# Memory rows kept without their token factor: the factor moves from GpSimd to the keys and values, and the key weights come as whole rows

## The chip, the core and the metric

The kernel runs on one core of a Trainium2 chip, as one launch. The core has a matrix engine (TensorE, PE in the profile, with PEld for its weight loads), VectorE (DVE), ScalarE (ACT), GpSimd (POOL) and a queue engine (SyncE, SP) that here issues almost all DMAs. The metric is the device time of one execution in microseconds, lower is better. Of several runs the median is compared.

## What is computed

One step of a two-layer encoder trunk on 512 prompt tokens and 32 sample tokens, model width 1024. Layer 0 mixes tokens by an RWKV-7 recurrence, layer 1 by differential attention. Both layers also attend to a memory of 256 rows, and what matters for the change is how the keys and values of that memory are made:

```python
def rmsnorm(x, w):
    xf = x.astype(jnp.float32)
    y = xf * lax.rsqrt(jnp.mean(xf * xf, axis=-1, keepdims=True) + EPS)
    return (y * w.astype(jnp.float32)).astype(x.dtype)

def mem_kv(mem, norm_w, wk, wv):
    h = rmsnorm(mem, norm_w)
    return ((h @ wk).reshape(B, N_MEM, MEM_HEADS, MEM_HD),
            (h @ wv).reshape(B, N_MEM, MEM_HEADS, MEM_HD))
```

For each layer `mem` is the same 256 x 1024 matrix `mem_prompt`; `norm_w`, `wk` and `wv` (1024 x 512, four heads of 128) are the layer's own. Keys and values are outputs as well as operands of the attention. The factor `rsqrt(mean(x*x) + EPS)` is one number for each memory row (for each token of the memory), the same for both layers: this is the token factor of the title. It stands in front of a whole row, so it can be applied to the row before the product with `wk` or `wv`, or to the product after it.

## The kernel before

Everything is kept transposed: features on the 128 partitions, tokens along the free axis, so a 1024-wide row is eight tiles, `k` = 0 to 7. The products of the two layers run in a split precision: a weight tile is cast by ScalarE to `whi`, VectorE forms the rest `wlo` = raw - `whi`, and activations are split into `hh` and `hl` in the same way (for the memory `mmh` and `mml`). Three matmuls (`whi` with `hh`, `whi` with `hl`, `wlo` with `hh`) make one product.

All instructions but those of GpSimd go through the helper class `Queue` (L99 to L104), so nearly every row of the profile names L104, and rows are told apart by tile names. While `self.ordered` is true, `Queue` ties each instruction of an engine behind the one that the program issued before it on that engine: in the opening, and in layer 0, the order of the program text is the order of each queue. SP's queue holds the DMAs in program order too. An instruction that waits holds up everything behind it on its engine.

The opening, `inputs()` (L363 to L563), does this, in the order of its text:

- It issues the loads: the memory rows `xm` in two halves (`memory(0)`, `memory(1)`), the norm weights `pB`, the key weights of layer 0 in eight pieces (`keys(g, k)`: 256 rows by 256 columns, that is two tiles `k` for the two heads of group `g`), the sample rows, the four prompt tiles `xp` (tiles `xt` 3 to 6 of the profile's numbering by `square` and `scaled`), then weight blocks (`load`, tile `raw`, five buffers) and small parameters.
- PE transposes the memory rows (`turn(k)`, tile `ps_mt`). `taken(k)` makes two copies: VectorE writes `m` (in buffer `at`), multiplied by the norm weight of layer 0, and ScalarE writes the plain copy `mo` (in `bv` and `yt`), which layer 1 will use with its own norm weight. Neither has the token factor yet.
- `key(g, k)` multiplies the key weights with `m` in plain float32: four matmuls of 128x256 each call (two tiles `k`, two heads), accumulated in four PSUM tiles, two heads first and the other two after.
- `square(i, ...)` sums the squares of the token rows (ScalarE or VectorE), `roots(v)` turns the sums into factors `rs` with nine short VectorE instructions in a row (L461 and `rsqrt`, L129), once for tiles 0 to 4 and once for tiles 5 and 6, the last two prompt tiles. `scaled(i, ...)` multiplies the prompt rows with their factors. The memory's factors are not put on the rows: two diagonal tiles `dg` and a matmul with ones spread them along the free axis, ScalarE copies them to `rb` (in `rsb`), and `key_out(h)` multiplies the finished keys of head `h` with `rb`.
- `turned(k)` transposes the scaled prompt tiles, `normed(k)` makes `hh` and `hl` from them (ScalarE, then VectorE), and a loop over `k` runs the first weight block (`raw36`) in step with them, with `mem_out` for the four heads of keys between.

Then layer 0 begins (`layer0`, L1413): `lora_in`, `memory()` (L565 to L578), and the first three ordinary blocks. `memory()` is where GpSimd comes in:

```python
            self.nc.gpsimd.tensor_tensor(x, x, r2, ALU.mult)
            self.ae.copy(mh[:, f, :], x)
            self.nc.gpsimd.tensor_tensor(ml[:, f, :], x, mh[:, f, :].bitcast(F32), ALU.subtract)
        for k in range(4):
            self.nc.gpsimd.tensor_tensor(mo[k], mo[k], r2, ALU.mult)
            self.se.dma_start(self.mscr[k], mo[k])
```

The eight multiplications by `r2` (L572, L576) put the factor on `m` and `mo`; four subtractions (L574) make `mml`; and `mo` goes out to DRAM (`mscr`). GpSimd's instructions aren't tied to the program order, so each starts as soon as its own operands are there, also in the middle of the opening. Later the values of layer 0 are made from `mmh` and `mml` (`mem_block`, L1167), `mem_again` (L1117) loads `mo` back for layer 1, and `mem_kv` (L1153) makes keys and values of layer 1. `mem_out` (L1139) transposes a finished head on PE, ScalarE copies it to `memt`, and SP stores it.

## Time and profile before

| what | us |
|---|---|
| median of 3 runs | 1441.03 |
| lowest and highest of them | 1439.93, 1441.11 |
| the profiled execution, its own time | 1438.12 |
| span of that execution, first to last instruction | 1436.4 |
| PE busy in the span | 1390.6 |
| DVE busy | 924.8 |
| ACT busy | 828.5 |
| POOL busy | 389.2 |

The profiled execution took 1438.12 us, 2.9 us less than the median, and 1.7 us of it lie outside the span. All times of the trace below belong to this one execution and count from the start of its span. A row of a timeline gives the start, the length, the engine, the tile written and the tiles read, the shape, how many instructions the row joins, and in brackets how long the engine stood idle before and what ended that.

### The profile page before, as it was taken

The numbers are of one execution on the slowest core, as the hardware profiler recorded it, in microseconds if no ns is written. First come the engines' busy times: TensorE is split into PE (matmuls) and PEld (weight loads), VectorE is DVE, ScalarE is ACT, GpSimd is POOL, SyncE is SP. The second block draws the span as 40 slices with busy tenths as digits, with TensorE's granted clock in tenths as the row PEclk, the third lists the DMA queues.
The fourth block names the chain that finished last, engine by engine and source line by source line (L and its number), as shares of the span: only waits on it lengthen the run. The fifth ranks groups of instructions, "written<-read, shape, count | busy, mean of one in ns | idle before, by whom it ended". The sixth has DMA issues, their size and how long they took to land.

```text
span 1436.4 us, 31914 instructions
## 1 busy us (share of the span) xinstructions
PE 1390.6 (97%) x11877; PEld 1310.1 (91%) x11877; DVE 924.8 (64%) x2337; ACT 828.5 (58%) x2278; POOL 389.2 (27%) x850
## 2 busy tenths in 40 slices
PE   6999999999999998999999999999999999999997
PEld 5998899999999998988999999989999999999997
DVE  6666777777877877676743656564465746557533
ACT  4665677767676676565433456654465446664322
POOL 4226567565765567600000120000000001000100
PEclk9999999999999999999999999999999999999999
DMA  6443222332223232342554472323332223332321
GB/s 206 125 129 88 58 58 73 82 97 59 78 76 82 75 78 60 92 122 77 165 160 127 142 206 68 91 85 96 97 90 82 85 74 89 90 105 59 97 83 70
DMA packets 264773, 139.20 MB, mean 97 GB/s; under 512 B 57689, under 2 KB 254562, under 8 KB 264618
## 3 DMA queue, kind: packets, MB, share of 16 engines
q1 hardware_dynamic: 264618, 137.16, 34.0%
q8 instruction: 94, 1.54, 0.4%
q14 instruction: 61, 0.50, 0.1%
HBM read 110.98 MB, written 22.78 MB: 93 GB/s over the span
## 4 chain that ended last, share of the span: by engine, by line
PE 81%; DVE 7%; ACT 7%; DMA 2%; issue 2%; SPq 1%; DVEq 0%; ACTq 0%
PE ps_g L104 56%; PE ps_c L104 4%; PE ps_s L104 2%; PE ps_o L104 2%; PE ps_at L104 2%; PE ps_v L104 1%; DVE wlo L104 1%; PE ps_mo L104 1%; PE ps_mm L104 1%; PE ps_aT L104 1%; SPq L104 1%; PE ps_ss L104 1%; ACT whi L104 1%; PE ps_w L104 1%; DVE nt L104 1%
## 5 line engine op out<-in xcount | busy, mean ns | idle before, releaser
L104 PE MATMUL ps_g<-hh,wlo 128*128 128x272 f32 x1808 | 538.3, 298 | 2.7 <-DVE wlo L104 2.7
L104 PE MATMUL ps_g<-hh,whi 128*128 128x272 f32 x1808 | 537.5, 298 | 0.6 <-DVE qp L104 0.6
L104 PE MATMUL ps_g<-hl,whi 128*128 128x272 f32 x1808 | 531.6, 295 | 0.3
L104 PEld LDWEIGHTS ps_g<-hh,wlo 128*128 128x128 f32 x1808 | 341.5, 189 | 7.5 <-DVE wlo L104 3.6
L104 PEld LDWEIGHTS ps_g<-hh,whi 128*128 128x128 f32 x1808 | 342.2, 190 | 5.0 <-PE ps_g L104 0.8
L104 PEld LDWEIGHTS ps_g<-hl,whi 128*128 128x128 f32 x1808 | 341.8, 189 | 4.5 <-DVE hl L104 0.7
L104 DVE TENSOR_TENSOR wlo<-raw,whi 128x512 fp32r<-128x512 f32 x314 | 218.7, 709 | 190.4 <-ACT whi L104 187.0
L104 ACT CAST whi<-raw 128x512 fp32r<-128x512 f32 x314 | 190.2, 617 | 173.1 <-PE ps_g L104 99.7
L860 POOL TENSOR_TENSOR tm<-u,m 102x84 f32<-102x84 f32 (+23 forms) x341 | 147.2, 432 | 155.4 <-DMA m<-sc 129.6
L862 POOL TENSOR_TENSOR u<-u,tm 102x84 f32<-102x84 f32 (+23 forms) x341 | 147.0, 431 | 26.6
L104 PE MATMUL ps_g<-hi,wlo 128*128 128x272 f32 x512 | 147.8, 289 | 0.9 <-DVE wlo L104 0.9
L104 PE MATMUL ps_g<-hi,whi 128*128 128x272 f32 x512 | 148.6, 290 | 0.0
L104 PE MATMUL ps_g<-lo,whi 128*128 128x272 f32 x512 | 147.4, 288 | 0.0
L1312 POOL TENSOR_TENSOR lo<-og,hi 128x544 fp32r<-128x544 f32 x8 | 13.7, 1713 | 486.4 <-DVE og L104 351.3
L104 PEld LDWEIGHTS ps_g<-hi,wlo 128*128 128x128 f32 x512 | 96.3, 188 | 1.1 <-DVE wlo L104 1.1
L104 PEld LDWEIGHTS ps_g<-hi,whi 128*128 128x128 f32 x512 | 96.4, 188 | 0.0
L104 PEld LDWEIGHTS ps_g<-lo,whi 128*128 128x128 f32 x512 | 96.4, 188 | 0.0
L104 DVE SCALAR_TENSOR_TENSOR SB<-ps_c,dl,sd 64x64 f32<-64x64 f32 x168 | 47.5, 283 | 41.3 <-PE ps_c L104 36.1
L1731 POOL TENSOR_TENSOR hl<-hn,hh 128x544 fp32r<-128x544 f32 x8 | 11.8, 1479 | 210.4 <-ACT hh L104 210.4
L104 ACT COPY sv<-ps_c 64x64 f32<-64x64 f32 x192 | 39.3, 205 | 44.4 <-PE ps_c L104 42.7
L104 ACT ACTIVATE sg<-ps_g 128x272 f32<-128x272 f32 x64 | 25.3, 395 | 64.1 <-PE ps_g L104 59.9
L104 ACT ACTIVATE pt<-ps_s,snm 128x128 f32<-128x128 f32 (+3 forms) x96 | 50.7, 529 | 18.0 <-DVE snm L104 17.0
(387 smaller groups left out, 2622.0 us busy)
## 6 DMA issues: line engine op xcount, KB each, us to landing
raw<-in_rw_in_dram SPq DMA_DIRECT2D x114, 256.0 KB
raw<-in_df_in_dram SPq DMA_DIRECT2D x112, 256.0 KB
raw<-in_w_out_dram SPq DMA_DIRECT2D x64, 256.0 KB
oscr<-sg SPq DMA_DIRECT2D x16, 272.0 KB
lo<-oscr SPq DMA_DIRECT2D x16, 272.0 KB
m<-sc SPq DMA_DIRECT2D x33, 128.0 KB
raw<-in_w_mem_v_dram SPq DMA_DIRECT2D x16, 256.0 KB
kh<-kh SPq DMA_DIRECT2D x24, 136.0 KB
```

The costliest lines, as they stand in the source:

```text
L104: return lambda *a, **k: self.trunk.tie(self, issue(*a, **k))
L860: nc.gpsimd.tensor_tensor(tm[:, :n, :wd], u3[:, :n, kx : kx + 1].to_broadcast(sh), m3[:, kx : kx + 1, kx + 1 :].to_broadcast(sh), ALU.mult)
L862: nc.gpsimd.tensor_tensor(u3[:, :n, kx + 1 :], u3[:, :n, kx + 1 :], tm[:, :n, :wd], ALU.add)
L1312: (self.nc.gpsimd if g % 2 and self.o1 else self.ve).tensor_tensor(lo[:], t, hi[:].bitcast(F32), ALU.subtract)
L1731: nc.gpsimd.tensor_tensor(self.hl[:, k, :], h[:], self.hh[:, k, :].bitcast(F32), ALU.subtract)
```

## The change

- The token factor no longer goes onto the memory rows. `memory()` loses the eight multiplications on GpSimd, and `m` and `mo` stay without the factor. `mml` is now subtracted by VectorE, in four instructions, in the order of the program.
- What is made from those rows gets the factor afterwards. Values (`mem_out` with `kind == 1`): memory tokens are on the partitions there, so ScalarE's copy of 128x256 becomes two activations of 128x128 with a factor for each partition (`self.mrs`, the tile `rs`, now kept in the constant pool). Keys of layer 1 (`mem_kv` with `kind == 0`): the copy out of PSUM, on ScalarE before, is a VectorE product with the spread factors `self.rsb`. Keys of layer 0 had `key_out` already.
- `rb` is stored to DRAM (`rscr`) in the opening, and loaded again in `mem_again`, after the eight tiles of `mo`.
- The stores of `mo` to `mscr` are issued at the end of `inputs()`, ahead of the loads `up`.
- The key weights come as eight pieces of 128 whole rows by 512 columns, and `key(k)` runs all four heads for one tile `k`. The loads of pieces 2 to 6 stand behind the sample rows, between and behind the prompt tiles. All four `key_out` now stand together behind `normed(0)`.
- The two loads of `pB` are issued first, and by ScalarE's queue.

```diff
-            def keys(g, k):
-                self.se.dma_start(wm[4 * g + k], a["w_mem_k"][0][2 * k * P : 2 * k * P + 2 * P, 2 * g * P : 2 * g * P + 2 * P]
-                                  .rearrange("(k p) c -> p k c", p=P))
+            def keys(*ks):
+                for k in ks:
+                    self.se.dma_start(wm[k], a["w_mem_k"][0][k * P : k * P + P, :])
...
+            parB = self.params(p, "pB", [(a[n].rearrange("l (j p) -> (l j) p", p=P), 16) for n in ("norm_w", "mem_norm_w")], self.ae)
             memory(0)
-            parB = self.params(p, "pB", [(a[n].rearrange("l (j p) -> (l j) p", p=P), 16) for n in ("norm_w", "mem_norm_w")])
-            keys(0, 0)
             keys(0, 1)
             memory(1)
-            keys(0, 2)
-            keys(0, 3)
             self.se.dma_start(xs[:TS, :], a["x_sample"][0])
             prompt(0)
+            keys(2)
             prompt(1)
-            keys(1, 0)
+            keys(3)
             prompt(2)
-            keys(1, 1)
+            keys(4)
             prompt(3)
-            keys(1, 2)
-            keys(1, 3)
+            keys(5, 6, 7)
...
-            ss, rs = (p.tile([P, 7], F32, name=n) for n in ("ss", "rs"))
+            ss, rs = p.tile([P, 7], F32, name="ss"), self.c.tile([P, 7], F32, name="rs")
+            self.mrs = rs
+            self.rscr = self.dp.tile([P, NMEM], F32, name="rscr")
...
-            key_out(0)
-            key_out(1)
             normed(0)
+            for h in range(MH):
+                key_out(h)
             todo[3][0]()
+            self.se.dma_start(self.rscr[:], rb)
...
-    def memory(self, m, mo, rb):
+            for k in range(4):
+                self.se.dma_start(self.mscr[k], mo[k])
+        return m
+
+    def memory(self, m):
 
         mh, ml = self.mem_tiles()
-        r2 = rb.unsqueeze(1).to_broadcast([P, 2, NMEM])
-        for k in range(4):
-            f = slice(2 * k, 2 * k + 2)
-            x = m[:, f, :]
-            self.nc.gpsimd.tensor_tensor(x, x, r2, ALU.mult)
-            self.ae.copy(mh[:, f, :], x)
-            self.nc.gpsimd.tensor_tensor(ml[:, f, :], x, mh[:, f, :].bitcast(F32), ALU.subtract)
-        for k in range(4):
-            self.nc.gpsimd.tensor_tensor(mo[k], mo[k], r2, ALU.mult)
-            self.se.dma_start(self.mscr[k], mo[k])
+        for k in range(0, KT, 2):
+            f = slice(k, k + 2)
+            self.ae.copy(mh[:, f, :], m[:, f, :])
+            self.ve.tensor_tensor(ml[:, f, :], m[:, f, :], mh[:, f, :].bitcast(F32), ALU.subtract)
...
-        self.ae.copy(tok[:], ps[:, :256].rearrange("p (j c) -> p j c", j=2))
+        if kind == 0:
+            self.ae.copy(tok[:], ps[:, :256].rearrange("p (j c) -> p j c", j=2))
+        else:
+            for j in range(2):
+                self.ae.activation(tok[:, j, :], ps[:, j * P : j * P + P], AF.Copy, scale=self.mrs[:, j : j + 1])
...
-            self.gemm([self.weights(src, h * P)], [(mh, ml)], lambda ps, v: self.ae.copy(t[:], ps), cols=NMEM, parts=1)
+            self.gemm([self.weights(src, h * P)], [(mh, ml)], lambda ps, v: self.ve.tensor_tensor(t[:], ps, self.rsb[:], ALU.mult)
+                      if kind == 0 else self.ae.copy(t[:], ps), cols=NMEM, parts=1)
```

What this does to GpSimd's own queue, from the end of its first memsets to the first pair's inversion. `at` holds `m`, `bv` and `yt` hold `mo`, `rsb` the spread factors. Before:

```order
L572 TENSOR_TENSOR at_89<-at_89,rsb 128x512
L576 TENSOR_TENSOR bv_94<-bv_94,rsb 128x512
L576 TENSOR_TENSOR bv_95<-bv_95,rsb 128x512
L572 TENSOR_TENSOR at_89<-at_89,rsb 128x512
L576 TENSOR_TENSOR bv_102<-bv_102,rsb 128x512
L576 TENSOR_TENSOR yt_101<-yt_101,rsb 128x512
L572 TENSOR_TENSOR at_89<-at_89,rsb 128x512 x2
L1430 MEMSET raw_479 128x1
```

And in the changed kernel, between the same two neighbours:

```order
L1570 MEMSET yt_101 128x128
L1430 MEMSET raw_485 128x1
L1430 MEMSET raw_486 128x1
L212 IOTA t_508 128x640
L257 MEMSET bk 128x32 x2
```

All eight products are gone, and nothing stands in their place on this queue.

VectorE's queue in the opening, from the sample rows' `hl` on, the lines with a minus before and those with a plus now; `memk` are the keys of layer 0 as `key_out` writes them, `hl<-ps_t` is VectorE's half of `normed(k)`:

```order
 L104 TENSOR_TENSOR hl<-rsb,hh 128x8x32
-L104 TENSOR_TENSOR memk<-ps_g,rsb 128x256 x2
 L104 SCALAR_TENSOR_TENSOR hl<-ps_t,PB,hh 128x512
-L104 TENSOR_TENSOR wlo<-raw,whi 128x512
-L104 SCALAR_TENSOR_TENSOR hl<-ps_t,PB,hh 128x512 x2
-L104 TENSOR_TENSOR memk<-ps_g,rsb 128x256
-L104 SCALAR_TENSOR_TENSOR hl<-ps_t,PB,hh 128x512
+L104 TENSOR_TENSOR memk<-ps_g,rsb 128x256 x3
 L104 TENSOR_TENSOR memk<-ps_x,rsb 128x256
-L104 SCALAR_TENSOR_TENSOR hl<-ps_t,PB,hh 128x512 x2
+L104 TENSOR_TENSOR wlo<-raw,whi 128x512
+L104 SCALAR_TENSOR_TENSOR hl<-ps_t,PB,hh 128x512 x5
```

The four key products are now one group behind the first `hl`, ahead of `wlo` and the second `hl`; before, two stood ahead of the first and two further back.

VectorE's queue at the start of layer 0, in the changed kernel:

```order
L104 SCALAR_TENSOR_TENSOR tmp<-raw_485,PA,tmp 128x544
L104 TENSOR_TENSOR wlo<-raw,whi 128x512
L104 TENSOR_TENSOR lora_574<-tmp,lora_574 64x544
L104 TENSOR_TENSOR lora_575<-tmp,lora_575 64x544
L104 TENSOR_TENSOR mml<-at_89,mmh 128x512 x4
L104 SCALAR_TENSOR_TENSOR rkv<-raw_486,PA,rkv 128x544
L104 TENSOR_TENSOR wlo<-raw,whi 128x512
```

The four `mml` are the new rows; before, `rkv` followed `lora` directly, and GpSimd made `mml` beside it.

More of the change, by code (lines that the diff above doesn't have):

```diff
@@ L141, in rsqrt, with params @@
         self.ve.scalar_tensor_tensor(y, t[:], 5.0 * f ** 4, y, ALU.add, ALU.mult)
-    def params(self, p, name, rows):
+    def params(self, p, name, rows, queue=None):
         t = p.tile([P, P], F32, name=name)
@@ L444, in taken, with key @@
                 self.ae.copy(mo[k], v)
-            def key(g, k):
-                for j in range(2):
-                    for h in range(2):
-                        self.te.matmul(pk[2 * g + h][:, :NMEM], wm[4 * g + k][:, j, h * P : h * P + P], m[:, 2 * k + j, :],
-                                       start=k + j == 0, stop=2 * k + j == KT - 1)
+            def key(k):
+                for h in range(MH):
+                    self.te.matmul(pk[h][:, :NMEM], wm[k][:, h * P : h * P + P], m[:, k, :], start=k == 0, stop=k == KT - 1)
             def square(i, act):
@@ L491, in inputs @@
             taken(1)
-            key(0, 0)
+            key(0)
             square(0, True)
@@ L496, in inputs @@
             taken(2)
-            key(0, 1)
+            key(1)
             turn(3)
             taken(3)
-            key(0, 2)
-            key(0, 3)
+            key(2)
+            key(3)
             square(2, True)
@@ L525, in inputs @@
             todo[2][0]()
-            key(1, 1)
+            key(5)
             ps = self.psm.tile([P, 512], F32, tag="m", name="ps_ts")
@@ L537, in inputs @@
             self.ve.tensor_tensor(self.hl[:, :, TP:], hs, self.hh[:, :, TP:].bitcast(F32), ALU.subtract)
-            key_out(0)
-            key_out(1)
             normed(0)
+            for h in range(MH):
+                key_out(h)
             todo[3][0]()
+            self.se.dma_start(self.rscr[:], rb)
             self.early = [self.load(w, 0)]
@@ L1121, in mem_again @@
         for k in range(KT + 2):
-            if k < KT:
-                mo[k] = p.tile([P, NMEM], F32, tag="memo", name="mo", bufs=2)
-                self.se.dma_start(mo[k][:], self.mscr[k // 2][:, k % 2, :])
+            if k <= KT:
+                t = p.tile([P, NMEM], F32, tag="memo", name="mo", bufs=2)
+                self.se.dma_start(t[:], self.mscr[k // 2][:, k % 2, :] if k < KT else self.rscr[:])
+                if k < KT:
+                    mo[k] = t
+                else:
+                    self.rsb = t
             if 0 < k <= KT:
```

15 lines of the change are left out of this document (6 added, 9 removed).

## The prediction

> **What bounds the kernel now.** I read the page first, then PE's waits, then the stretches of the opening with the granted clock, then the timelines of PE, DVE, POOL and ACT there. The page says that PE is the engine to watch:
>
> ```profile
> span 1436.4 us, 31914 instructions
> PE 1390.6 (97%) x11877; PEld 1310.1 (91%) x11877; DVE 924.8 (64%) x2337; ACT 828.5 (58%) x2278; POOL 389.2 (27%) x850
> ```
>
> PE is idle for 1436.4 - 1390.6 = 45.8 us. A change that leaves PE's work as it is can win only from these, and from work that PE does at a low clock. The list of PE's waits names the largest (us in total, times, longest):
>
> ```profile
> PE ps_t L104 <- DVE xt L104: 6.4, 1, 6.4
> PE ps_g L104 <- DVE wlo L104: 3.6, 5, 1.1
> ```
>
> The first is one wait, for VectorE's scaled prompt tile. The table by stretches (length, then busy time of PE, PEld, DVE, ACT, POOL, then PE's granted clock, DMA share, GB/s) shows it, and what it costs afterwards:
>
> ```profile
> 24.00:30.19 6.19, 0.00 (x1) 0.01 (x1) 5.95 (x9) 0.81 (x1) 4.93 (x5) 0.69 0.17 50
> 30.19:34.00 3.81, 3.81 (x14) 3.23 (x15) 3.34 (x8) 2.42 (x5) 0.00 (x0) 0.60 0.33 103
> ```
>
> PE does nothing for 6.2 us, and in the 3.8 us after it the clock is 0.60. Why is VectorE late? Its timeline:
>
> ```profile
> 19.27 1.21 DVE L104 SCALAR_TENSOR_TENSOR sg<-xt 128x1024 f32<-128x1024 f32 x1
> 20.59 1.05 DVE L104 TENSOR_SCALAR ss<-ss 128x2 f32<-128x2 f32 x1
> 21.67 1.19 DVE L104 TENSOR_SCALAR rs<-ss 128x2 int32<-128x2 int32 x1
> ...
> 27.77 1.18 DVE L104 TENSOR_TENSOR nt<-nt,ss 128x2 f32<-128x2 f32 x1
> 28.99 0.16 DVE L104 SCALAR_TENSOR_TENSOR nt<-nt 128x2 f32<-128x2 f32 x1
> 29.18 0.16 DVE L104 SCALAR_TENSOR_TENSOR rs<-nt,rs 128x2 f32<-128x2 f32 x1
> 29.38 0.75 DVE L104 TENSOR_SCALAR xt<-xt,rs 128x1024 f32<-128x1024 f32 x1
> ```
>
> Nine instructions on two columns each make the factors of the last two prompt tiles. The last two take 0.16 us, the seven before them 1.05 to 1.19. POOL's timeline says what runs beside the slow ones:
>
> ```profile
> 19.81 1.79 POOL L572 TENSOR_TENSOR at<-at,rsb 128x512 f32<-128x512 f32 x1 [11.61 <-ACT rsb L104]
> 21.57 2.48 POOL L576 TENSOR_TENSOR bv<-bv,rsb 128x512 f32<-128x512 f32 x2
> ...
> 27.68 1.25 POOL L572 TENSOR_TENSOR at<-at,rsb 128x512 f32<-128x512 f32 x1
> ...
> 55.85 5.98 POOL L574 TENSOR_TENSOR mml<-at,mmh 128x512 fp32r<-128x512 f32 x4 [2.31 <-ACT mmh L104]
> ```
>
> From 19.81 to 28.93 POOL multiplies rows with the token factor, 1.25 us each, and each short DVE instruction lasts about as long as one of them, as if one were let through for each of POOL's. When POOL stops, DVE is back at 0.16. These are the instructions that the change removes.
>
> **Term 1, the gap.** What is next when POOL is silent? DVE's nine start at 20.59 and follow each other by 29.38 - 29.18 = 0.20 us: done at 22.4. DVE then scales one tile (0.75, to 23.2) and ACT the other:
>
> ```profile
> 18.13 1.15 ACT L104 ACTIVATE xt<-xt,rs 128x1024 f32<-128x1024 f32 x1 [0.30 <-DVE rs L104]
> ```
>
> that is to 23.6. PE's own timeline:
>
> ```profile
> 12.56 3.62 PE L104 MATMUL ps_g<-at,at 128*128 128x256 f32 x16
> ...
> 18.64 0.68 PE L104 MATMUL ps_rb<-dg,ones 128*128 128x128 f32 x4 [0.74 <-DVE dg L104]
> ...
> 23.43 0.38 PE L104 MATMUL ps_t<-ident,xt 128*128 128x128 f32 x2
> 30.19 1.72 PE L104 MATMUL ps_t<-ident,xt 128*128 128x128 f32 x6 [6.38 <-DVE xt L104]
> ```
>
> PE has key products until 23.43, so DVE and PE now arrive together, and PE goes on at about 23.8 instead of 30.19. Gain 6.4.
>
> **Term 2, the clock.** Without the gap the clock should stay at 1.00. PE's 3.81 us at 0.60 hold 3.81 x 0.60 = 2.3 us of work: gain 1.5.
>
> [...]
>
> **Term 3, the second collision.** At 55.85 POOL makes `mml`, and DVE is slow again; PE stands:
>
> ```profile
> 48.13 0.68 DVE L104 TENSOR_TENSOR wlo<-raw,whi 128x512 fp32r<-128x512 f32 x1
> ...
> 57.46 1.53 DVE L104 SCALAR_TENSOR_TENSOR rkv<-raw,PA,rkv 128x544 f32<-128x544 f32 x1 [1.50 <-ACT raw L104]
> 58.91 1.77 DVE L104 TENSOR_TENSOR wlo<-raw,whi 128x512 fp32r<-128x512 f32 x1
> ```
>
> ```profile
> 60.74 0.39 PE L104 MATMUL ps_g<-hh,wlo 128*128 128x272 f32 x1 [1.13 <-DVE wlo L104]
> ```
>
> `wlo` takes 1.77 us instead of 0.68. The change gives DVE the four subtractions itself. They have the form of `wlo` (128x512, both inputs in SBUF), 0.6 each back to back, and each waits for its cast:
>
> ```profile
> 55.15 2.19 ACT L104 CAST mmh<-at 128x512 fp32r<-128x512 f32 x4
> ```
>
> They begin when the second `lora` is done, 55.96, and end near 58.4. Behind them queue `rkv` and `wlo`, 0.7 each: 59.8 instead of 60.69. PE waits about 0.2 instead of 1.13: gain 0.9. If DVE were slowed by something else there it could be 0; it can't exceed 1.13.
>
> **Term 4, the keys in a bunch.** `key_out` times four stands ahead of the second `hl`. With PE starting its first `whi` step at 26.1 (23.8, six transposes 0.6, four key products 1.7), `key_out(3)` ends near 27.1, `wlo` 27.7, the second `hl` 28.4, where PE wants it at 27.6. Part comes back, since DVE has no key product inside the loop any more and the third `hl` comes at the same distance from the start as before (3.0 us): cost 0.4, between -0.5 and 0.8.
>
> **Term 5, the order of the loads.** Key rows 3 and 4 now follow prompt tiles 1 and 2. Those land here:
>
> ```profile
> 14.70 1.23 DVE L104 SCALAR_TENSOR_TENSOR sg<-xt 128x1024 f32<-128x1024 f32 x1 [1.25 <-DMA xt<-in_x_prompt_dram]
> ```
>
> ```profile
> 16.68 1.06 ACT L104 ACTIVATE junk<-xt 128x1024 f32<-128x1024 f32 x1 [0.40 <-DMA xt<-in_x_prompt_dram]
> ```
>
> Ahead of row 3 stand as many bytes as before ahead of prompt tile 1, so it lands near 14.7. PE (16 key matmuls from 12.56 are rows 2 and 3) wants it at 14.3. Row 4 lands near 16.7, wanted at 16.0. PE slips by 0.4 to 0.7, but it stands for 0.74 before `ps_rb` anyway. Cost 0.2, at most 1.1. No transfer grows; rows are 2 KB instead of 1.
>
> **Term 6, the small ones.** `pB` by ACT's queue is issued 0.9 us earlier, but PE waits only this long for it:
>
> ```profile
> 5.67 0.28 PE L104 MATMUL ps_par<-ident,pB 32*128 32x32 f32 x1 [0.22 <-DMA pB<-in_mem_norm_w_dram]
> ```
>
> Gain 0.2, between 0 and 0.22. On SP's queue the four `mscr` stores now pass ahead of `up`, some 2.5 us of issuing; `up` is wanted ten microseconds later, and the stores wait for nothing: 0. `rscr` is one issue ahead of a weight load, 0.35 us, waiting for `rb`, long there: 0. Each of eight `memt` becomes two instructions:
>
> ```profile
> L104 ACT COPY memt<-ps_mkt 128x256 f32<-128x256 f32 x16 | 5.9, 371 | 7.3 <-DMA mkv<-memt 3.8 <-PE ps_mkt L104 3.4
> ...
> L104 ACT ACTIVATE osT<-ps_osT,dv 128x128 f32<-128x128 f32 x3 | 1.1, 367 | 1.6 <-PE ps_osT L104 1.6
> ```
>
> At most 0.36 us more each, 2.9 together, on an engine that is 58% busy, and only a store waits for it. Cost 0.1, between 0 and 0.7.
>
> **Term 7, layer 1's keys.** Here the change adds waits: four `memx` on DVE, each held until PE has finished its block, with the whole DVE queue behind. DVE is nearly full there. Two of its groups, 816 to 834, while POOL makes `hl` (count, then busy us, mean ns, then idle before):
>
> ```profile
> L104 DVE TENSOR_TENSOR wlo<-raw,whi 128x512 fp32r<-128x512 f32 x11 | 11.0, 1032 | 0.4 <-ACT whi L104 0.4
> L104 DVE SCALAR_TENSOR_TENSOR hn<-x,PB,ps_r 128x512 f32<-128x512 f32 x8 | 5.9, 738 | 0.3 <-POOL hl L1731 0.3
> ```
>
> `hl` of the opening has `hn`'s form with POOL nearly silent, and `x`, from 760 to 811, has `memx`'s, one input in PSUM and one in SBUF:
>
> ```profile
> L104 DVE SCALAR_TENSOR_TENSOR hl<-ps_t,PB,hh 128x512 fp32r<-128x512 f32 x8 | 6.0, 748 | 5.7 <-ACT hh L104 5.5
> ```
>
> ```profile
> L104 DVE TENSOR_TENSOR x<-ps_g,x 128x272 f32<-128x272 f32 x8 | 3.5, 438 | 6.2 <-PE ps_g L104 6.2
> ```
>
> Beside POOL `wlo` goes from 0.68 to 1.03 us, and `hn`, at 738 against 748 ns, isn't slowed. I take 0.42 for each `memx`; slowed like `wlo` it would be 0.63. That is 1.7 to 2.5 us more on an engine that `wlo` and `hn` alone fill for 16.9 of 18 us. One of the four falls into this idle time, one into the 0.4 before `wlo`:
>
> ```profile
> 811.95 0.17 DVE L104 TENSOR_SCALAR tm_m<-ps_n 128x5 f32<-128x5 f32 x1 [1.03 <-PE ps_n L104]
> ```
>
> The other two push the rest by 0.4 each, and I put half of that on PE. Cost 0.4, between 0 and 2.
>
> [...]
>
> **The sum.** 6.4 + 1.5 + 0.9 + 0.2 - 0.4 - 0.2 - 0.1 - 0.4 = 7.9 us. After 62 us PE is the bound, and everything there is released by PE's progress, so I expect the shift to be kept to the end. The profiled execution's 1438.12 would be 1430.2. It was 2.9 below the median of the runs; taking the sum off the median, 1441.03 - 7.9 = 1433.1.
>
> **Rivals.**
> 1. *The loads set the opening.* If the rows 4 to 7, now last, come 3 to 4 us late, PE waits for `zr` instead of `xt`: gain 4.4, 1436.6. For it: the loads run at full share to 20 us; against: PE never waits for a key row now, and byte counts don't grow. 0.12.
> 2. *Layer 1's DVE queue, slower than before.* ACT's copies of these products, which DVE now makes, follow their blocks, some 3 us each (the third and the fourth):
>
> ```profile
> 820.10 0.37 ACT L104 COPY memx<-ps_g 128x256 f32<-128x256 f32 x1
> ...
> 822.65 0.37 ACT L104 COPY memx<-ps_g 128x256 f32<-128x256 f32 x1
> ```
>
> If each `memx` holds DVE for a whole block and PE then stands for `wlo`, four times 3 us and 0.8 for slowing make 12.8, net 4.9 slower: 1446. It decides from 7.9 us of PE idle between 811 and 835. Against it: in DVE's queue `memx` stands about where its block ends, so it should wait for tenths. 0.04.
> 3. *Given back.* If layer 0's stages are paced by weights or by SP's queue and not by PE, the opening's gain turns into waiting for `raw` before 130 us: 1441. Against: from 62 to 70 PE is full. 0.06.
> 4. *More.* The bunch of keys costs nothing, the loads with whole rows come faster, and the first loop, where DVE has less to do, shortens by 2: gain 11, 1430. 0.08.
>
> **The numbers.** The forecast has 0.70. The range reaches from 1429.0 (gain 10.5, and 1.5 for the spread of the runs shown, 3 us with the profiled one) to 1438.0 (rival 1 and 1.4 of spread); it leaves out rivals 2 and 3. A measurement of this kernel can tell about 0.2%, 2.9 us, from no change. Faster by more than that: forecast, rivals 1 and 4, 0.90; within it: rival 3, 0.06; slower: rival 2, 0.04.
>
> **What would show it.** In the profile after: the nine instructions at 0.16 to 0.2 each; no wait of PE for `xt` above 1 us; clock 1.00 from 24 to 34; the first `whi` step near 26; `wlo` at 0.7 near 50; PE idle in the layer-1 stage below 2 us. I am wrong if PE waits there for `zr`, `raw` or `wlo` instead, if the nine stay slow with POOL silent, or if the first 100 us are 8 us shorter and the end isn't.

## The result, and the profile after

The changed kernel takes 1433.11 us (median of 4 runs, 1432.36 to 1433.81) against 1440.55 (4 runs, 1439.93 to 1441.11): ratio 0.9948, 95% interval 0.9931 to 0.9966, 7.4 us less. The profiled execution took 1432.36. Of all runs below, one of experiment 6 took 1499.98 us at a granted clock of 0.847 and is left out of its ratio. Its page, in the lines that answer to those of before:

```profile
span 1430.4 us, 31910 instructions
PE 1391.5 (97%) x11877; PEld 1309.5 (92%) x11877; DVE 917.7 (64%) x2345; ACT 828.8 (58%) x2282; POOL 375.0 (26%) x838
```

PE's idle time fell from 45.8 to 38.9 us. In the list of PE's waits the largest of before, `xt` with 6.4, is gone; this line stands:

```profile
PE ps_g L104 <- DVE wlo L104: 3.3, 6, 0.9
```

VectorE's timeline has the nine short instructions (first and last) and the prompt tile behind them, PE's timeline the transposes of it and the first step of the loop; the last line is the first step before:

```profile
20.19 0.17 DVE L104 TENSOR_SCALAR ss<-ss 128x2 f32<-128x2 f32 x1
...
21.77 0.16 DVE L104 SCALAR_TENSOR_TENSOR rs<-nt,rs 128x2 f32<-128x2 f32 x1
21.96 0.75 DVE L104 TENSOR_SCALAR xt<-xt,rs 128x1024 f32<-128x1024 f32 x1
```

```profile
18.24 0.68 PE L104 MATMUL ps_rb<-dg,ones 128*128 128x128 f32 x4 [0.21 <-DVE dg L104]
...
23.02 1.04 PE L104 MATMUL ps_t<-ident,xt 128*128 128x128 f32 x8
...
25.94 0.63 PE L104 MATMUL ps_g<-hh,whi 128*128 128x272 f32 x2 [0.16 <-DVE memk L104]
```

```profile
34.01 0.60 PE L104 MATMUL ps_g<-hh,whi 128*128 128x272 f32 x2
```

The nine take 1.7 us instead of 8.8. PE makes eight transposes of the prompt tiles without a wait and begins the loop at 25.94, where before it began at 34.01. The table by stretches (columns as in the prediction) shows the granted clock, the seventh figure after the busy times, at 1.00:

```profile
24.00:26.00 2.00, 1.84 (x10) 1.32 (x8) 1.71 (x4) 1.26 (x3) 0.00 (x0) 1.00 0.26 78
26.00:30.00 4.00, 3.67 (x27) 3.36 (x28) 2.80 (x6) 1.34 (x2) 0.00 (x0) 1.00 0.78 228
```

The second collision, on VectorE's timeline:

```profile
48.53 2.50 DVE L104 TENSOR_TENSOR mml<-at,mmh 128x512 fp32r<-128x512 f32 x4
50.94 0.78 DVE L104 SCALAR_TENSOR_TENSOR rkv<-raw,PA,rkv 128x544 f32<-128x544 f32 x1
51.64 0.69 DVE L104 TENSOR_TENSOR wlo<-raw,whi 128x512 fp32r<-128x512 f32 x1
```

To see where the gain is kept and where it is lost, the starts of PE's instructions in the two traces were matched one by one (same tiles, same count); the table gives start after minus start before, at the time that the place had before:

| place before, us | 34.01 | 46.6 | 58 | 60 to 68 | 104 | 160 | 180 | 264 | 800 | 836 to 848 | 852 | end |
|---|---|---|---|---|---|---|---|---|---|---|---|---|
| after minus before | -8.07 | -7.45 | -7.47 | -8.35 | -7.62 | -8.29 | -5.64 | -5.41 | -6.97 | -5.50 | -6.05 | -5.94 |

Three steps back after 60 us have to be explained: 0.73 between 68 and 104, 2.65 between 160 and 180, 1.47 between 800 and 836. Of the 0.67 gained between 104 and 160 nothing can be given to the change: the kernel before, profiled a second time (10, below), gains as much there on its first profile. The first step back is a wait at ScalarE's two-piece `memt` (ScalarE's and PE's timelines):

```profile
62.36 0.62 ACT L104 ACTIVATE memt<-ps_mkt,rs 128x128 f32<-128x128 f32 x2
```

```profile
63.03 0.39 PE L104 MATMUL ps_wa<-lora,uh 128*128 128x272 f32 x1 [0.24 <-ACT memt L104]
```

In the second, 0.25 is a wait for `t1b`, which VectorE makes in the second pair's merge, that grew from 0.74 to 0.98; the other 2.4 has no wait. The stretches tell what it is, the clock:

```profile
164.00:168.00 4.00, 2.86 (x43) 2.48 (x43) 2.92 (x11) 0.78 (x3) 0.00 (x0) 0.67 0.51 135
168.00:172.00 4.00, 4.00 (x19) 4.00 (x19) 0.53 (x3) 1.79 (x7) 2.68 (x11) 0.50 0.52 145
```

The third is VectorE's lateness in layer 1 (PE's waits between 800 and 850):

```profile
PE ps_mkt L104 <- DVE memx L104: 0.6, 1, 0.6
PE ps_g L104 <- DVE wlo L104: 0.5, 1, 0.5
```

### The profile page after: what moved, and what is told of

It is laid out like the page before. It is cut to its first block, busy times and chain, and to the rows that moved or that the text cites. A ratio compares the mean times of both kernels' runs of the same rounds, so it can differ in the third digit from the quotient of the medians.

```text
span 1430.4 us, 31910 instructions
## 1 busy us (share of the span) xinstructions
PE 1391.5 (97%) x11877; PEld 1309.5 (92%) x11877; DVE 917.7 (64%) x2345; ACT 828.8 (58%) x2282; POOL 375.0 (26%) x838
## 4 chain that ended last, share of the span: by engine, by line
PE 82%; DVE 8%; ACT 6%; issue 2%; DMA 1%; SPq 1%; DVEq 0%; ACTq 0%
PE ps_g L104 57%; PE ps_c L104 4%; PE ps_s L104 2%; PE ps_o L104 2%; PE ps_at L104 2%; DVE wlo L104 1%; PE ps_v L104 1%; PE ps_mo L104 1%; PE ps_mm L104 1%; PE ps_aT L104 1%; SPq L104 1%; PE ps_yc L104 1%; PE ps_ss L104 1%; ACT whi L104 1%; PE ps_w L104 1%
## 5 line engine op out<-in xcount | busy, mean ns | idle before, releaser
L1731 POOL TENSOR_TENSOR hl<-hn,hh 128x544 fp32r<-128x544 f32 x8 | 12.7, 1588 | 212.9 <-ACT hh L104 212.7
```

The costliest lines, as they stand in the source:

```text
L1731: nc.gpsimd.tensor_tensor(self.hl[:, k, :], h[:], self.hh[:, k, :].bitcast(F32), ALU.subtract)
```

## The experiments

The theory: the gain is GpSimd's silence (*silence*). Rivals: it is the order of the loads (*loads*), or the removed instructions held others up by their results (*dependency*). Then come the late costs, one by one. Ratios are to the kernel before, timed on the same chip. One thing has to be taken off first. PE's first matmuls are slow in the profiles of before (both), the changed kernel, x2 and x3, as eight key matmuls early and eight a little later in the first profile of before show:

```profile
6.97 3.15 PE L104 MATMUL ps_g<-at,at 128*128 128x256 f32 x8
...
10.39 1.89 PE L104 MATMUL ps_g<-at,at 128*128 128x256 f32 x8
```

The trace's records of the granted clock at 1.00 begin at 9.34 us there and at 8.33 in the changed kernel. The first eight key matmuls take 3.78 us in x2 and in the second profile of before and 3.75 in x3, and `pB`, for which PE waits ahead of its second four transposes, lands up to 1.4 us later in some. So PE comes to `ps_rb` (the matmul with ones that spreads the memory's factors) at 18.64 before, and at 18.24, 19.76, 19.46 and 21.00 in the others, and all of this lies ahead of GpSimd's first product (19.81 before). This offset is named where it matters, and distances within the opening are counted from `ps_rb`.

**1. GpSimd's work put back, without its results (x1_pool_back).**

```diff
             self.ae.copy(rb, ps[:, :NMEM])
+            sink = p.tile([P, 2, NMEM], F32, name="sink")
+            r2 = rb.unsqueeze(1).to_broadcast([P, 2, NMEM])
+            for k in range(8):
+                self.nc.gpsimd.tensor_tensor(sink[:], mo[k % 4], r2, ALU.mult)
```

> The changed kernel with eight GpSimd multiplications of the removed shape (128x512, both inputs in SBUF) put back at the place of the removed ones; they write a tile that nobody reads, so only GpSimd's being busy comes back, no dependency. Silence theory (the gain is that GpSimd is quiet while VectorE makes the factors): the short VectorE instructions take 1.05 to 1.2 us again instead of 0.16, PE waits about 6 us for xt, the first whi step moves from 25.9 to about 34, and the whole gain is lost: ratio to the kernel before 0.9995, between 0.998 and 1.001. Dependency theory (the removed instructions cost because other work waited for their results): nothing waits for these, first whi step at 26, ratio 0.995. Loads theory (the gain is the order of the loads, which stays): first whi step at 26, ratio 0.995.

Measured: 1441.16 us, ratio 1.0005 (0.9996 to 1.0013). The whole gain is gone. GpSimd's, VectorE's and PE's timelines:

```profile
19.51 4.56 POOL L515 TENSOR_TENSOR sink<-bv,rsb 128x512 f32<-128x512 f32 x3 [11.30 <-ACT rsb L104]
```

```profile
21.37 0.17 DVE L104 TENSOR_SCALAR rs<-ss 128x2 int32<-128x2 int32 x1
21.57 1.14 DVE L104 SCALAR_TENSOR_TENSOR nt<-rs 128x2 f32<-128x2 f32 x1
22.75 0.16 DVE L104 TENSOR_TENSOR nt<-nt,ss 128x2 f32<-128x2 f32 x1
22.94 1.15 DVE L104 SCALAR_TENSOR_TENSOR rs<-nt,rs 128x2 f32<-128x2 f32 x1
...
26.80 1.86 DVE L104 TENSOR_SCALAR xt<-xt,rs 128x1024 f32<-128x1024 f32 x1
```

```profile
28.72 1.54 PE L104 MATMUL ps_t<-ident,xt 128*128 128x128 f32 x6 [5.22 <-DVE xt L104]
```

Nothing reads `sink`, the loads are the new ones, and yet PE waits 5.22 us for `xt` again: silence holds, loads and dependency fall as the main cause. Only every second short instruction is slow here (five of nine, against seven before), so the first loop step comes at 32.98, not 34; why the pattern differs stays open.

**2. The kernel before, with the eight multiplications left out (x2_before_silent).** The values, and the keys of layer 1, come out without the token factor; `key_out` still puts it on the keys of layer 0.

```diff
-            self.nc.gpsimd.tensor_tensor(x, x, r2, ALU.mult)
             self.ae.copy(mh[:, f, :], x)
...
-            self.nc.gpsimd.tensor_tensor(mo[k], mo[k], r2, ALU.mult)
             self.se.dma_start(self.mscr[k], mo[k])
```

> The kernel before with its eight GpSimd multiplications by the token factor left out (so keys and values of the memory come out without it) and nothing else changed: loads, key weights, the four mml on GpSimd, one copy for each memt, ACT's memx all as before. Silence theory: the nine short VectorE instructions at 0.16 us, first whi step at 25.5 to 26.5, 7.9 us gained in the opening and neither the 0.9 of mml nor the losses at memt and memx: ratio 0.9945, between 0.993 and 0.996. Loads theory: the opening is as before or gains under 2 us, ratio above 0.998.

Measured: 1431.74 us, ratio 0.9937 (0.9925 to 0.9948): silence alone brings as much as the whole change, or more. The first step of the loop on PE's timeline:

```profile
26.96 0.60 PE L104 MATMUL ps_g<-hh,whi 128*128 128x272 f32 x2
```

That is later than expected, but PE's work from the third transposes on stands 1.12 behind before's; without this offset it is 25.84. From `ps_rb` to this step PE takes 7.20 us, where it took 15.37 before: silence alone is worth 8.17 there.

**3. The loads of before (x3_old_loads).**

```diff
-            def keys(*ks):
-                for k in ks:
-                    self.se.dma_start(wm[k], a["w_mem_k"][0][k * P : k * P + P, :])
+            def keys(g, k):
+                self.se.dma_start(wm[4 * g + k], a["w_mem_k"][0][2 * k * P : 2 * k * P + 2 * P, 2 * g * P : 2 * g * P + 2 * P]
+                                  .rearrange("(k p) c -> p k c", p=P))
...
```

The rest of the edit puts the loads of the key pieces back into the old order (in the change, pieces 2 to 7 stand between and behind the prompt tiles), `pB` back on SP's queue, and the key products back to two heads at a time.

> The changed kernel with the loads of before: key weights in 2 x 128 x 256 pieces by pairs of heads, in the old order among the prompt tiles, pB on SP's queue, key products two heads at a time. Silence theory: first whi step between 25.4 and 26.5, ratio 0.9948, between 0.994 and 0.9958. Loads theory: most of the gain goes, first whi step after 28, ratio above 0.997.

Measured: 1435.02 us, ratio 0.9962 (0.9949 to 0.9975), a little above the range of silence, far below 1. The first step comes at 27.16, with an offset of 0.82. From `ps_rb` to it PE takes 7.70 us, exactly as in the changed kernel, and from the third transposes of the memory rows to `ps_rb` 6.53, as there and in every other profile (6.52 or 6.53). So behind the first 12 us the order of the loads is worth nothing. PE's wait ahead of `ps_rb` did shrink from 0.74 to 0.21 us in the changed kernel, but only because PE came later to it, by 0.53 in all, waiting for key rows. What is left is the start of the opening, up to `ps_rb`; it varies by itself (18.24 to 19.46 with the new loads, 18.64 to 21.00 with the old), and whether the new order has a part in it, and in the 1.9 us between the two medians, the profiles don't settle.

**4. mml on GpSimd again (x4_mml_pool).**

```diff
-            self.ve.tensor_tensor(ml[:, f, :], m[:, f, :], mh[:, f, :].bitcast(F32), ALU.subtract)
+            self.nc.gpsimd.tensor_tensor(ml[:, f, :], m[:, f, :], mh[:, f, :].bitcast(F32), ALU.subtract)
```

> The changed kernel with the four mml subtractions on GpSimd again. Second-collision theory: they start near 48, wlo beside them takes 1.7 us instead of 0.69, PE waits about 1.1 us for it at about 52, and from 60 on PE runs 0.9 us later than in the changed kernel: ratio 0.9954. If wlo is late there for another reason (its cast, its weights), PE's place at 60 stays within 0.3 us and the ratio at 0.9948.

Measured: 1435.06 us, ratio 0.9962 (0.9949 to 0.9975). VectorE's and PE's timelines:

```profile
52.01 1.76 DVE L104 TENSOR_TENSOR wlo<-raw,whi 128x512 fp32r<-128x512 f32 x1
```

```profile
53.83 0.39 PE L104 MATMUL ps_g<-hh,wlo 128*128 128x272 f32 x1 [1.15 <-DVE wlo L104]
```

PE's distance from before is -6.92 at 58 and -6.92 at 60, where the changed kernel goes from -7.47 to -8.35: 0.88 us, as the theory has it.

**5. One copy for memt (x5_memt_copy).** The token factor of the values is left out, in both layers.

```diff
-        if kind == 0:
-            self.ae.copy(tok[:], ps[:, :256].rearrange("p (j c) -> p j c", j=2))
-        else:
-            for j in range(2):
-                self.ae.activation(tok[:, j, :], ps[:, j * P : j * P + P], AF.Copy, scale=self.mrs[:, j : j + 1])
+        self.ae.copy(tok[:], ps[:, :256].rearrange("p (j c) -> p j c", j=2))
```

> The changed kernel with the eight memt of the values made by one ACT copy each, as before (their token factor is left out, so the memory's values come out without it). Tile theory: the two activations in a row hold PE's PSUM tile ps_mkt 0.25 us longer, and the next product waits for it; PE's loss between 62 and 104 is under 0.25 us here where the changed kernel loses 0.74, and the ratio falls by 0.0004. Store theory, the prediction's: only a store waits for memt, PE loses the same 0.74 us there for another reason.

Measured: 1432.65 us, ratio 0.9947 (0.9934 to 0.996), too wide for half a microsecond; but PE's distance is -7.14 at 68 and -7.13 at 104. The 0.73 is `memt`'s, and the store theory falls. ScalarE's copy:

```profile
63.57 0.36 ACT L104 COPY memt<-ps_mkt 128x256 f32<-128x256 f32 x1
```

**6. Two key_out back into the loop (x6_keyout).**

```diff
+            key_out(0)
+            key_out(1)
             normed(0)
-            for h in range(MH):
-                key_out(h)
...
+                if k in (1, 2):
+                    key_out(k + 1)
```

> The changed kernel with two key_out ahead of the first normed and the other two inside the loop, as before. Bunch theory: PE's loop of the first projection shortens by the 0.4 to 0.6 us that it lost (steps from the first whi to ps_par pA take 12.6 to 12.8 us instead of 13.2), time 0.4 us less. If the order of key_out doesn't matter, since the third hl comes no sooner, the loop stays at 13.2.

Measured: 1432.38 to 1435.49 us in four runs, ratio 0.9954 (0.9941 to 0.9968), no difference that the times can tell. PE's timeline of this run:

```profile
25.86 0.59 PE L104 MATMUL ps_x<-at,zr 128*128 128x256 f32 x2
26.10 0.60 PE L104 MATMUL ps_g<-hh,whi 128*128 128x272 f32 x2
```

The loop, from the first `whi` step to `ps_par` of `pA`, takes 13.01 us (26.10 to 39.11), against 13.24 in the changed kernel (25.94 to 39.18), 12.62 before (34.01 to 46.63) and 12.84 in x2. That is 0.23, about half of what was expected. But the bunch also costs ahead of the loop, where the expectation didn't look: here the first step follows `ps_rb` (18.91) by 7.19 us, as in x2 and x11 (7.20), which have two `key_out` ahead of the first `normed` as well; in the changed kernel and every one that keeps the bunch and GpSimd's silence it is 7.70 or more. There the step starts 0.75 us after the last key product and not 0.24 (25.86 to 26.10), and the row of the changed kernel says what it waits for, VectorE's `memk`: `key_out` reads the keys out of the PSUM tiles `ps_g`, of which there are three, and the first step needs two of them. So the bunch costs 0.74 from `ps_rb` to `pA` (20.94 against 20.20 us), nearly twice the forecast. The loop is 0.2 to 0.4 longer than before also without it (x2, x6, x11), for a reason that stays open.

**7. ACT's memx (x7_memx_act).** The token factor of layer 1's keys is left out.

```diff
-            self.gemm([self.weights(src, h * P)], [(mh, ml)], lambda ps, v: self.ve.tensor_tensor(t[:], ps, self.rsb[:], ALU.mult)
-                      if kind == 0 else self.ae.copy(t[:], ps), cols=NMEM, parts=1)
+            self.gemm([self.weights(src, h * P)], [(mh, ml)], lambda ps, v: self.ae.copy(t[:], ps), cols=NMEM, parts=1)
```

> The changed kernel with layer 1's four memx of the keys copied by ACT, as before (layer 1's memory keys come out without the token factor). Queue theory: the loss of 0.9 us that PE takes between 811 and 855 (it waits for wlo, and for memx) is gone, PE runs there within 0.2 us of its distance at 800. If the loss belongs to the shift in time itself (another order of loads against compute), it stays at 0.9.

Measured: 1431.54 us, ratio 0.994 (0.9926 to 0.9953). PE's distance is -6.09 at 800 and -6.25 at 848: the 1.47 are gone. (Near 850 the later profiles, but x3, gain 0.4 to 0.8 on the first one of before, a second profile of before as well: that one had a wait of its own there.)

**8. GpSimd writes but doesn't read (x1b_pool_memset).**

```diff
             self.ae.copy(rb, ps[:, :NMEM])
+            sink = p.tile([P, 2, NMEM], F32, name="sink")
+            one = self.nc.gpsimd.tensor_copy(sink[:, 0, :], rb)
+            for k in range(16):
+                two = self.nc.gpsimd.memset(sink[:], 0.0)
+                self.order(two, one)
+                one = two
```

> The changed kernel with one GpSimd copy and sixteen GpSimd fills of a 128x512 tile put where the removed multiplications were: GpSimd writes SBUF and reads nothing. Busy theory (any GpSimd work beside VectorE slows it): while the fills run, from about 19.5 to at least 27, the short VectorE instructions take as long as one fill each, and the first whi step moves by over 2 us. Read theory (it is GpSimd's reading of two SBUF inputs that counts): they stay at 0.16 to 0.2 us and the first whi step at 25.4 to 26.7.

Measured, one run: 1434.33 us. GpSimd's and VectorE's timelines:

```profile
21.38 9.69 POOL L515 MEMSET sink<- 128x512 f32 x16
```

```profile
21.38 0.55 DVE L104 TENSOR_SCALAR rs<-ss 128x2 int32<-128x2 int32 x1
21.96 0.16 DVE L104 SCALAR_TENSOR_TENSOR nt<-rs 128x2 f32<-128x2 f32 x1
...
23.33 0.87 DVE L104 TENSOR_SCALAR xt<-xt,rs 128x1024 f32<-128x1024 f32 x1
```

The first of the nine is done before the fills begin; of the eight beside them seven take 0.16 us. Only two TENSOR_SCALARs are longer, the one shown first by 0.4 and the scaling of the prompt tile by 0.1, and the first step follows `ps_rb` by 8.18 us, 0.48 more than in the changed kernel (it is at 27.41, or 26.4 without an offset of 0.99 against that kernel). So GpSimd's being busy and its writing cost at most this 0.48 us; what the multiplications have beyond the fills is that they read SBUF (and that they compute, which no run here separates).

**9. Both late costs mended in a first way (x8_best).**

```diff
+        elif i == 0:
+            self.ve.tensor_tensor(tok[:], ps[:, :256].rearrange("p (j c) -> p j c", j=2),
+                                  self.mrs[:, :2].unsqueeze(2).to_broadcast([P, 2, P]), ALU.mult)
         else:
             for j in range(2):
...
             yield
+            if kind == 0:
+                self.ve.tensor_tensor(t[:], t[:], self.rsb[:], ALU.mult)
```

with ACT's copy in `mem_kv` as in 7.

> The changed kernel with both late costs mended: the values' memt of layer 0 by one VectorE multiplication with the factor instead of two activations, and layer 1's four memx copied by ACT again and multiplied in place one block later, so that VectorE waits for no product. Everything is computed. If tile theory and queue theory hold, PE loses under 0.25 us between 62 and 104 (0.74 in the changed kernel) and gains between 811 and 855 what it gained with the copies alone (0.88, where the changed kernel lost 0.91): about 2 us less than the changed kernel, ratio 0.9935. If VectorE's work itself (not its waiting) is the cost in layer 1, only the first 0.5 us come.

Measured: 1434.96 us, ratio 0.9959 (0.9946 to 0.9973): not better than the changed kernel. `memt` on VectorE loses 0.64 between 68 and 104, nearly as much as the two activations. And layer 1 loses 1.9 in one place (VectorE's and PE's timelines):

```profile
816.57 1.56 DVE L104 TENSOR_TENSOR memx<-memx,mo 128x256 f32<-128x256 f32 x1
```

```profile
818.27 0.41 PE L104 MATMUL ps_mkt<-ident,memx 128*128 128x128 f32 x2 [2.11 <-DVE memx L104]
```

(`mo` stands for the spread factors, which lie in a buffer of that tile.) Multiplied in place, `memx` has both inputs in SBUF; beside GpSimd's `hl` it takes 1.56 us, and 0.42 at 806.63, where GpSimd stands idle. The changed kernel's form, one input in PSUM, took 0.41 there. The attempt removed a wait and bought a collision.

**10. The kernel before once more (x10_before).** Nothing is edited.

> The kernel before once more, for a second profile of it. Sparse-PE theory with chance in it: the clock falls in two or three stretches of 3 to 8 us again, one of them at 24 to 34, the others not all where the first profile had them (264 and 584); PE's places agree with the first profile to 0.5 us between such stretches. If the stretch at 172 to 180, which every changed kernel shows and the first profile of before does not, belongs to the change, it is missing here too.

Measured, one run: 1441.64 us. Its stretches at the place in question, and where the first profile had a fall:

```profile
176.00:180.00 4.00, 3.10 (x41) 2.83 (x41) 2.89 (x12) 0.76 (x3) 0.16 (x1) 0.57 0.71 187
180.00:184.00 4.00, 4.00 (x21) 4.00 (x21) 0.63 (x3) 2.16 (x7) 3.06 (x13) 0.57 0.41 103
264.00:268.00 4.00, 4.00 (x35) 3.87 (x32) 2.31 (x7) 3.21 (x11) 0.00 (x0) 1.00 0.39 114
```

Here the unchanged kernel has the fall at the second pair's merge, 2.7 us of it, and none at 264 or 584. The fall isn't the change's.

**11. Filler at that place (x9_fill).**

```diff
         ps = self.psx.tile([P, 512], F32, tag="x", name="ps_w1")
+        if st["pr"] == 1:
+            for _ in range(5):
+                self.te.matmul(ps[:, :P], self.ones[:], self.ident[:], start=True, stop=True)
```

> The changed kernel with five 128x128 matmuls on constants put in the second pair's merge, where PE stands 0.98 us for t1b; their result is overwritten. Sparse-PE theory (the clock falls to 0.50 from 166 to 172 because PE had too little work just before): the clock stays at 1.00 there and PE's place at 180 is 2.0 to 2.9 us earlier against its place at 160 than in the changed kernel; ratio 0.9935. If the clock falls on its own schedule, it is at 0.50 there or a few us later all the same, and PE loses up to 0.9 us more for the five.

Measured: 1431.91 us, ratio 0.9937 (0.9925 to 0.995). PE's timeline and the stretches:

```profile
165.09 1.28 PE L104 MATMUL ps_w<-ident,ones 128*128 128x128 f32 x10
166.30 0.24 PE L104 MATMUL ps_w<-t1b,at 32*32 32x32 f32 x2
```

```profile
164.00:168.00 4.00, 3.84 (x57) 3.57 (x58) 2.88 (x10) 1.13 (x4) 0.20 (x1) 1.00 0.41 115
168.00:172.00 4.00, 4.00 (x61) 3.85 (x59) 2.11 (x9) 3.23 (x10) 3.14 (x12) 1.00 0.57 157
```

PE's distance is -8.22 at 160 and -7.99 at 180: 0.23 lost, to the later `t1b`, where the changed kernel loses 2.65. Of the twelve profiles without filler nine show the fall there (x2 has one at 132 to 144 instead), of the two with it none; the mean granted clock of the five runs is 0.996 to 0.998, of the changed kernel's four 0.994 to 0.996. That speaks for sparse PE as the cause, and the count in the last section bears it out. Some 1.7 us were still lost to a fall at 256 to 264 (clock 0.68, then 0.90).

**12. All four late costs mended (x11_all).** With the edits of 6, 7 and 11, and:

```diff
+                rsb = p.tile([P, NMEM], F32, tag="memx", name="memr", bufs=2)
+                self.se.dma_start(rsb[:], self.rscr[:])
...
+                self.ve.tensor_tensor(mo[j][:], mo[j][:], rsb[:], ALU.mult)
                 self.ae.activation(mh[:, j, :], mo[j][:], AF.Copy, scale=w[:, j : j + 1])
...
+        self.ae.copy(tok[:], ps[:, :256].rearrange("p (j c) -> p j c", j=2))
+        if kind == 1 and i == 0:
+            for j in range(2):
+                self.ae.activation(tok[:, j, :], tok[:, j, :], AF.Copy, scale=self.mrs[:, j : j + 1])
```

> The changed kernel with all four late costs mended, everything computed: two key_out ahead of the first normed and two in the loop; layer 0's memt copied from PSUM in one piece and multiplied by the factor afterwards in SBUF, so that PE's tile is free after the copy; five matmuls on constants in the second pair's merge; and layer 1's rows multiplied by the token factor when they are read back (740 to 800, where VectorE has room), so that keys and values there are plain copies by ACT. If the four theories hold, PE's loop keeps what the opening won (under 0.1 us lost, 0.6 in the changed kernel), loses under 0.25 us between 62 and 104 (0.74), runs at clock 1.00 from 160 to 180, and loses under 0.3 us between 811 and 848 (1.47): about 4 us less than the changed kernel, 1429, ratio 0.992, with up to 2 of it taken back where the clock falls elsewhere. If the mended costs only move (VectorE late at 740 to 800, ACT late at 62 to 104), ratio 0.9945 as the changed kernel.

Measured: 1427.38 us (1426.98 to 1429.12), ratio 0.9921 (0.9906 to 0.9936), the best of all. Layer 1 loses nothing (-9.80 at 800, -9.95 at 848): the factor on the rows costs 0.42 us eight times where VectorE has room (groups of 735 to 800):

```profile
L104 DVE TENSOR_TENSOR mo<-mo,memr 128x256 f32<-128x256 f32 x8 | 3.3, 418 | 0.3 <-DMA mo<-mscr 0.3
```

The clock is 1.00 in every stretch of 4 us from 16 to 368 and from 792 to 1152, and 0.998 in the mean of the span (0.994 in the changed kernel). Two parts failed. The loop takes 12.99 us and not 12.7, as in 6. And `memt` loses 0.77 between 68 and 104, as much as before its mending. PE's two waits for `memt` at `ps_wa` (0.4 us in the changed kernel) are gone, but others stand in their place, the first at this row:

```profile
66.52 0.44 PE L104 MATMUL ps_mkt<-ident,memx 128*128 128x128 f32 x2
```

It comes when ScalarE's next copy, `memx`, ends (66.12 + 0.35), and that copy starts 4.96 us after the one before it, against 4.27 with one copy for `memt` (5) and 4.53 in the changed kernel: from the start of `memt` to its next work ScalarE now takes 1.0 us, against 0.3 and 0.5. So the cost has two ways to PE, the PSUM tile that is held and ScalarE's later work, and this attempt closed one and widened the other.

## Why the prediction was right, point by point

The forecast 1433.1 met 1433.11. The mechanism that carries it, the short instructions freed from GpSimd, is shown by 1 and 2. That the number fits to the hundredth is luck: the kernel before took 1440.55 this time, not the 1441.03 that the sum was taken from, and by the traces the terms come to 6.1 only; what fills that up to 7.4 is in none of them.

- **Term 1, the gap, and term 2, the clock**, 7.9 together and the first step forecast at 26.1: it came at 25.94, 8.07 earlier. Of these 0.40 stood already at `ps_rb`; silence is worth 8.17 (2), and the bunch takes 0.50 back. Shown by 1 (the work put back alone takes all of it away) and 2 (left out alone, it gives all). In term 2 the 1.5 us are right for the opening (the second profile of before lost 2.0). What it didn't see: the clock falls in other places as well, in one to three stretches of each profile but the last (in those of the experiments, between 0 and 368 and between 792 and 1152 us), and differently in each. The first profile of before lost (busy time times what is missing to 1.00) 4.8 us so, 3.3 of them at 264 and 584; the one after 4.5, at 164 and 576. Outside the opening that is 1.2 more than before lost, most of the way from 5.8 us, the difference of the two profiles, to the 7.4 of the medians.
- **Term 3, the second collision**, 0.9: 0.88 in the traces, and 4 gives it back. Right, and by the path described.
- **Term 4, the bunch**, 0.4: 0.74 (6), 0.50 of it ahead of the loop. What the term left out is a wait: the first `whi` step was taken to follow the key products at once, at 26.1, but it waits for `key_out`, which frees its tile. The bound of 0.8 held.
- **Term 5 and pB in term 6**, 0 together. The mechanism of term 5 was right: PE slipped by 0.53 us for key rows (0.4 to 0.7 forecast), and the wait ahead of `ps_rb` took it in, wholly, so the cost was 0 and not 0.2. For `pB` the bound of 0.22 was one profile's: x2 waited 0.53 and the second profile of before 1.47.
- **Term 6, memt**, 0.1: 0.73. Here a step failed, "only a store waits for it". `memt` also frees the PSUM tile `ps_mkt`, one of two, and PE's next `ps_wa` waited for it (5 takes the loss away); 12 shows that ScalarE's own time counts as well. The 0.7 at the bound's end was the answer.
- **Term 7, layer 1's keys**, 0.4: 1.47 (7). The mechanism, work pushed back on a nearly full VectorE, is what PE waits for (0.6 for a `memx` itself, 0.5 for `wlo`); the size was off: the prediction put half of two pushes on PE, and 1.47 is nearly all of four times 0.42.
- **Rivals.** The loads didn't set the opening. Layer 1's queue did cost, but 1.5 and not the 7.9 that it needed. "Given back" didn't happen by `raw` or SP. "More", a gain of 11, didn't come: the bunch cost, and the loop grew by 0.62 instead of shortening by 2. (12 gains 12.5 by its medians, by other edits.)

By the traces the terms make 8.07 - 0.62 + 0.88 - 0.73 - 1.47 = 6.1 us, 1.8 less than forecast; the medians show 7.4. The 1.3 between them is about one fall of the clock; that it is one was not shown.

What stands beside GpSimd's work on VectorE comes to this. `memx` takes 0.42 us from PSUM at 812.02 in the changed kernel, inside GpSimd's `hl`, and 1.56 from SBUF beside it (9). `wlo`, with both inputs in SBUF, takes 0.68 us alone and 1.77 beside `mml` in the kernel before. Beside fills (8) seven of eight short instructions take 0.16 and two TENSOR_SCALARs are longer. Two inputs in SBUF are not the whole condition: the TENSOR_SCALARs `ss` and `rs`, with one tile as input, took 1.05 and 1.19 us beside GpSimd's multiplications in the kernel before. What the condition is was not shown.

## What to carry to other kernels

When a row of tiny instructions on VectorE takes about as long each as the GpSimd instruction beside it (here 1.05 to 1.19 us beside 1.25), look at that instruction as the cost: here multiplications into a tile that nobody reads cost as much as those that were wanted (1441.16 us against 1440.51), and fills 0.48 us; that it is the reading of SBUF was not shown apart from the computing. Count what waits behind that row, and move the work or wait it out. Ask of each instruction that is made longer or moved back not only who reads its output but which buffer it frees; that was missed twice here, at `memt` and at `key_out`. And give a factor that may be applied at several places to the place where an engine has room, not to the one where the data happens to be at hand: the same multiplication cost 1.5 us at layer 1's keys and nothing on the rows that they are made from, at 740 to 800.

## What the runs showed of the hardware

The granted clock falls to 0.50 for 3.4 or 6.8 us at a time (3.41 at 265 and 6.83 at 26 in the kernel before, 6.83 at 165 and 3.41 at 578 in the changed kernel) also where PE is hardly idle: in the 3.41 us ahead of the fall at 265 before, PE was busy for 3.35. Which of several places is hit differs between runs of one kernel (264 and 584 in one profile of before, 176 in the other), at 1.7 to 3.4 us of PE's work each. It goes with the spread between runs: the runs of experiment 5 go from 1430.14 us at a mean clock of 0.997 to 1435.14 at 0.993.

The traces of the kernel before and of the changed kernel also say which places are hit. In each the changes of the clock lie whole multiples of 3.41 us apart (before, the falls at 26.41, 265.34 and 586.20 us are 70 and 94 of them apart), and this grid lies differently in the two. Count the columns that PE's matmuls stream in the 3.41 us ahead of each point of the grid, weighted with the rows and columns that they use as a part of 128*128 (plain float32 twice, since 256 columns take 0.216 us there and 272 of the split products 0.126), as a share of a stretch full of split products. Of these 824 stretches at clock 1.00 the five with a share up to 0.33 were all followed by a fall, two of the four from 0.34 to 0.37, and none of the other 815, with 0.41 and more. PE's busy time doesn't tell them apart: ahead of the fall at 265 before, PE was busy for 98%, but partly with matmuls of two columns or on a 32*32 part, and the share was 0.31; ahead of 490 in the changed kernel it was busy for 98% as well, with 0.45 and no fall. Ahead of 165 the share is 0.33 in the changed kernel (a fall) and, by an estimate from PE's timeline and the place of the fall at 256 to 264, 0.47 in experiment 11 (no fall), with the two grids about 0.1 us apart; half of the difference are the added matmuls, half the products that this 0.1 us brings in. No run was made to test this count.
